# A decoder layer on one core: a third pair in seven products in three more units, with part of the low halves made by DMA

## The chip, the cores and the metric

One core of a Trainium2 chip runs one launch of the whole layer. The metric is the device time of that launch in microseconds (us).

## What is computed

```python
# x: 1 x 256 x 2048, fp32; D_MODEL 2048, SEQ 256, D_FF 5632
xn = rms(x)
p  = xn @ w_in                                   # all columns of both mixers, gates included
h  = x + (sigmoid(gA) * (fox(p) @ w_up_fox) + sigmoid(gB) * (nsa(p) @ w_up_nsa)) @ w_out
y  = h + (silu(rms(h) @ w_ffn_gate) * (rms(h) @ w_ffn_up)) @ w_ffn_down
```

FoX is attention with a forget gate (8 heads); NSA is attention with compressed, selected and windowed keys. The change touches the start of the program, the product with `w_out`, and the first of the three groups of `w_ffn_down`.

## The kernel before

**Products in two halves.** All is fp32 to the last digits: each operand is split into a high part `hi` (rounded by ACT) and a low part `lo` (the rest, by DVE), and one product of 128x128 by 128x512 is three matmuls: high by high (L1167), high by low (L1168), low by high (L1169). The attention part has the same in L199 to L201.

**Pairs.** From the merge gates on, the work is a list of items, each a `Pair`: 256 rows of a weight by 1024 columns (two tiles of 128 rows, two halves of 512 columns). SP loads it raw (`load`, L1116), `split` (L1119 to L1145) makes its high and low parts, and PE multiplies it with the transposed activations. A plain pair takes 8 products, which is 24 matmuls (`mm_plain`). A pair whose number is in `sevens` takes 7 products, 21 matmuls, by Strassen's scheme in Winograd's form (`mm_seven`, banks m1 to m7). For these DVE makes sums of the weight's quarters (L1126, L1128, L1129) and two low parts (L1145), and ACT two high parts (L1143, L1136). A pair in `thin` has the low part of its second half made without DVE: ACT writes minus the high part into `lo` (L1138), and a DMA that POOL issues adds the weight onto it from memory (L1139); DVE makes the other half, 128x1024.

**Units.** `unit` (L1174) takes an order of eight pairs (six in the first group of `w_ffn_down`) that add up in the same banks of the PSUM. There are four "acc" banks, handed out in turn, for m1, m5, m6, m7 and for transposes, and four "m" banks for the rest. After the last pair in seven products `combine` (L1204) takes the acc banks to SBUF, with ACT and DVE (L1209 to L1213); after the last item `last` adds the m banks (L1223) and `done` takes the result on. `hooks` names work that goes in front of an item, (j, 0), or into the middle of a plain one, (j, 1).

**Transposes.** Activations are transposed on PE (L1084, four of 128x128 a pair) into an acc bank. `put_plain` takes the bank out for a plain pair: ACT writes the high part (L1044), DVE the low (L1045). `put_seven` does so for a pair in seven products, with sums: three passes of ACT (L1060, L1066, L1073) and five of DVE (L1067, L1069, L1070, L1071, L1076). `put_m` transposes for `w_out`, `hid_pair` for `w_ffn_down`.

**Order.** Each engine does its instructions in the order of the program. `run_ffn` keeps three raw pairs and four split parts ahead, and places loads and splits at an item's start and half way through an item in seven products. Nothing sets the order but this code and the tables that the change edits: `ORDER` and `THIN` (L1406 to L1408), `SD` (L1347), the call of `unit` for `w_out` (L1337 to L1341) and its hooks. `swiglu` sets its product (`mult`, L1363) two items later, `down` the store of a second unit three items later, as DMAs that add into `hacc` in memory (L1378).

**Start.** `awake(n)` (L249) multiplies the identity with itself n times, for PE to be at work before its operands are there; then come the first transposes (`transpose_gain`, L279) of x and the first products of the attention part (L199 to L201).

Of the kernel before, what the change touches and what calls it, by code (L numbers as in the profile page):

```python
# [9 lines left out]
F32R = mybir.dt.float32r  # L10
# [4 lines left out]
P = 128  # L15
# [39 lines left out]
def hybrid_block(ctx: ExitStack, tc: tile.TileContext, x, norm_attn, w_in, fox_f_bias,  # L55
# [193 lines left out]
    def awake(n):  # L249

        tp = bank("tp")
        for _ in range(n):
            nc.tensor.matmul(tp[:, 0:P], ident, ident, start=True, stop=True)

    awake(5)
    tp = bank("tp")
    nc.tensor.transpose(tp[:, 0:16], vna, ident[:16, :16])
    nc.vector.tensor_copy(vecT[:, 0:16], tp[:, 0:16])
# [666 lines left out]
    mT = [None] * 8  # L925
    msrc = {}
    here = [0]
# [84 lines left out]
    def home(key, kp, sevens):  # L1012

        four = len(sevens) == 4
        if four and key == 1:
            if kp in sevens:
                halves[key, kp] = u8(ypool, [P, 2, 8, P], F32R)
                return halves[key, kp][:, :, 0:7]  # L1020
            if kp == 7:
                return tuple(halves[key, o][:, :, 7] for o in sevens)
        if kp in sevens:
            return u8(ypool, [P, 2, 8, P], F32R)
        if four:
            return p3([P, 2, 2, T], "hp", 4, F32R) if kp == 7 else p3([P, 2, 2, T], "x4", 3, F32R)
        if kp == 4:
            return u8(ypool, [P, 2, 2, T], F32R)
        if kp in (1, 3):
            if (key, 1) not in halves:  # L1030
                halves[key, 1] = u8(ypool, [P, 2, 2, 2, T], F32R)
            return halves[key, 1][:, kp // 2]
        return p3([P, 2, 2, T], "x4", 3, F32R)
# [209 lines left out]
    def two(w, r0, c0):  # L1243
        return lambda kp: [w[r0 + kp * 2 * P:r0 + (kp + 1) * 2 * P, c:c + 512] for c in (c0, c0 + 512)]
# [45 lines left out]
    def put_m(kp, where):  # L1290
# [3 lines left out]
                                    kp % 2 * 256, kp, SW, where=where)  # L1294
        return put

    SX = (0, 1, 2, 3)
    unit((4, 5, 0, 6, 1, 2, 3, 7), (0, 1, 3), two(w_in, 0, OFF_GA + 1024), x_pair((0, 1, 3)), ga_evac(1),
         thin=(6, 7))
# [20 lines left out]
    def put_hs(kp, j):  # L1320

        return {(j + o // 2, o % 2): lambda o=o: put_h(kp + o) for o in range(4)}

    def h_evac(i):
        def done(c):
            hs[i] = dict(c)
            for t, h in ((0, 0), (1, 0), (0, 1), (1, 1)):
                row_ssq(hss[:, t, 2 * i + h:2 * i + h + 1], c[t, h])
                nc.gpsimd.dma_start(hacc[t * P:(t + 1) * P, (2 * i + h) * 512:(2 * i + h + 1) * 512], c[t, h])
        return done  # L1330
# [4 lines left out]
        rstd_from(rh, s2[:, :NT], D)  # L1335

    for i in range(2):  # L1337
        unit(range(8) if i else (1, 3, 0, 2, 5, 6, 4, 7), SW if i else SW[:2], two(w_out, 0, i * 1024),
             lambda kp: mT[kp], h_evac(i),
             put_hs(0, 5) if i else {(1, 0): put_m(5, "acc"), (1, 1): put_m(6, "acc"), (4, 1): put_m(4, "acc"),  # L1340
                                     (5, 1): put_m(7, "acc")}, add_rows(x, i * 1024))  # L1341


    hid = {}
    hsrc = {}
    GROUPS = ((0, 3), (3, 7), (7, 11))
    SD = ((0, 2), (0, 2, 4, 6), (0, 2, 4, 6))  # L1347

    def hid_pair(f, a, g):
        f0, f1 = GROUPS[g]  # L1350
# [18 lines left out]
    def down(g, i):  # L1369
        final = g == len(GROUPS) - 1  # L1370

        def store(c):
            for t, h in ((0, 0), (1, 0), (0, 1), (1, 1)):
                rows, cols = slice(t * P, (t + 1) * P), slice((2 * i + h) * 512, (2 * i + h + 1) * 512)
                if final:
                    nc.sync.dma_start(out[rows, cols], c[t, h])
                else:
                    nc.gpsimd.dma_start(hacc[rows, cols], c[t, h], accum_op=ALU.add)  # L1378

        def done(c):  # L1380
            if final or not i:
                store(c)
            else:
                after.append((here[0] + 3, lambda c=dict(c): store(c)))
        return done, add_rows(hacc, i * 1024) if final else None

    def transposes(f, j):

        return {j if isinstance(j, tuple) else (j, 1): lambda: [hid_pair(f, o, g_of[f]) for o in range(2)]}
# [7 lines left out]
    def down_unit(g, i, order, hooks, thin=()):  # L1397
# [5 lines left out]
             lambda kp: hid[f0 + kp // 2, kp % 2], done, hooks, add, thin, True)  # L1403

    g_of = {f: g for g, (f0, f1) in enumerate(GROUPS) for f in range(f0, f1)}
    ORDER = ((range(6), range(6)), ((0, 7, 2, 1, 4, 3, 6, 5), (0, 7, 2, 1, 4, 6, 3, 5)),  # L1406
             ((0, 1, 2, 4, 3, 5, 6, 7), (0, 1, 2, 4, 3, 6, 5, 7)))
    THIN = (((), ()), ((3, 5), (3, 5)), ((1,), ()))  # L1408
    for g, (f0, f1) in enumerate(GROUPS):
        more = g + 1 < len(GROUPS)  # L1410

        for f in range(f0 + (1 if g else 0), f1 + (1 if more else 0)):
            gate_up(f, transposes(f - 1, (7, 0)) if f > f0 + (1 if g else 0) else
                    {} if f else {(2, 0): h_rms, **put_hs(4, 3)})
        hooks = ({}, transposes(f1, 6 if g else 4)) if more else (transposes(f1 - 1, 4), {})
        for o in range(2):
            down_unit(g, o, ORDER[g][o], hooks[o], THIN[g][o])

# [10 lines left out]
    def split_next():  # L1429
        nonlocal nsplit  # L1430
        split(stream[nsplit])
        nsplit += 1
        if nsplit == 1:
            transpose_gain(xT[0], xin, 0, VA, (0, 1))

    def run_att(i, ch):
        nonlocal nload
# [121 lines left out]
```

## Time and profile before

| | |
|---|---|
| runs (us) | 1415.89, 1417.41, 1419.33; median 1417.41 |
| the profiled execution | 1419.76 us, its span 1418.0 us |
| PE busy | 1409.3 us, 99% of the span |
| DVE, ACT busy | 1206.9 us (85%), 854.0 us (60%) |
| POOL busy | 121.5 us (9%) |
| weights and activations by SP's queue | 273.77 MB, 59.0% of the 16 DMA engines' time |
| by POOL's queue | 35.47 MB, 14.5% |

Busy shares are means over the program. PE works nearly without a pause, so the time is the sum of what PE is given plus its short waits; the other engines count only where PE waits for them. In the timelines a matmul of 128x512 shows some 0.39 us from issue to its end, but the next starts 0.227 us after it: what it costs is the distance of two starts.

### The profile page before, as it was taken

To read this page: it belongs to the slowest core of one execution; us is meant where nothing else is said; L and a number is where in the kernel's file an instruction comes from. 1 tells how busy PE (TensorE), PEld (TensorE's weight loads), DVE (VectorE), ACT (ScalarE), POOL (GpSimd) and SP (SyncE) were. 2 spreads that over 40 slices of the span, in tenths; PEclk is the share of its full clock that TensorE was granted. 3 is DMA by queue.
4 is the path that set the end of the run, shared out by engine and by line. 5 is a ranking of instruction groups with operands and counts; after the bars stand their busy time and mean duration, and the time that the engine had idled before them with its cause. 6 is when DMAs were issued, how large, how long until landed. Compare 5 with 4: busy or idle time off the path is not lost.

```text
span 1418.0 us, 18071 instructions
## 1 busy us (share of the span) xinstructions
PE 1409.3 (99%) x6507; PEld 1165.4 (82%) x6507; DVE 1206.9 (85%) x1566; ACT 854.0 (60%) x1080; POOL 121.5 (9%) x126
## 2 busy tenths in 40 slices
PE   9999999999999999999999999999999999999998
PEld 7888878888888888888888888888888888788887
DVE  5687877777767897879898999898999998899996
ACT  5556554556666665655665666556666666666643
POOL 0111000000000000100110000002010011110000
PEclk9999999999999999999999999999999999999999
DMA  7677877454434798777777778689878698978785
GB/s 261 202 222 204 262 244 211 137 165 136 147 119 149 248 256 253 202 229 233 226 226 233 212 237 264 203 223 284 226 238 252 200 242 256 264 230 248 222 243 158
DMA packets 177142, 310.67 MB, mean 219 GB/s; under 512 B 12910, under 2 KB 42188, under 8 KB 176924
## 3 DMA queue, kind: packets, MB, share of 16 engines
q1 hardware_dynamic: 159100, 273.77, 59.0%
q0 software_dynamic: 17776, 35.47, 14.5%
q8 instruction: 51, 0.84, 0.2%
q10 hardware_dynamic: 176, 0.27, 0.1%
q14 instruction: 39, 0.32, 0.1%
HBM read 301.07 MB, written 8.40 MB: 218 GB/s over the span
## 4 chain that ended last, share of the span: by engine, by line
PE 81%; DVE 7%; issue 6%; DMA 4%; ACT 1%; POOL 0%; SPq 0%; DVEq 0%; POOLq 0%; ACTq 0%
PE m L1168 11%; PE m L1167 11%; PE m L1169 11%; PE acc L199 9%; PE acc L201 9%; PE acc L200 9%; PE acc L1167 4%; PE acc L1168 4%; PE acc L1169 4%; DVE lo L1145 3%; DMA raw<-in_w_ffn_down_dram 2%; PE m L558 1%; DVE sums L1126 1%; DMA raw<-in_w_ffn_up_dram 1%; PE acc L1084 1%
## 5 line engine op out<-in xcount | busy, mean ns | idle before, releaser
L1145 DVE TENSOR_TENSOR lo<-raw,hi 128x1536 fp32r<-128x1536 f32 (+2 forms) x168 | 299.9, 1787 | 26.8 <-ACT hi L1141 14.3
L1143 ACT ACTIVATE hi<-raw 128x1536 fp32r<-128x1536 f32 (+1 forms) x125 | 208.1, 1668 | 87.4 <-PE m L1169 40.3
L175 DVE TENSOR_TENSOR hl<-raw,hl 128x1024 fp32r<-128x1024 f32 (+2 forms) x157 | 187.5, 1202 | 74.4 <-ACT hl L174 72.6
L1136 ACT ACTIVATE hi<-sums 128x1024 fp32r<-128x1024 f32 x154 | 161.3, 1060 | 147.5 <-PE m L1169 59.5
L199 PE MATMUL acc<-hl,u 128*128 128x512 f32 (+1 forms) x544 | 217.2, 399 | 0.2
L201 PE MATMUL acc<-hl,u 128*128 128x512 f32 (+1 forms) x544 | 212.2, 390 | 0.0
L200 PE MATMUL acc<-hl,u 128*128 128x512 f32 (+1 forms) x544 | 211.6, 389 | 0.0
L174 ACT ACTIVATE hl<-raw 128x1024 fp32r<-128x1024 f32 (+2 forms) x157 | 160.5, 1042 | 62.7 <-PE acc L201 48.3
L1145 DVE TENSOR_TENSOR lo<-sums,hi 128x2048 fp32r<-128x2048 f32 x77 | 175.9, 2284 | 5.9 <-ACT hi L1136 5.7
L1168 PE MATMUL m<-lo,hp 128*128 128x512 f32 x368 | 143.8, 391 | 2.3 <-DMA lo<-in_w_ffn_up_dram 2.0
L1167 PE MATMUL m<-hi,hp 128*128 128x512 f32 x368 | 144.1, 392 | 0.0
L1169 PE MATMUL m<-hi,hp 128*128 128x512 f32 x368 | 143.3, 389 | 0.0
L1167 PE MATMUL m<-hi,u 128*128 128x512 f32 x321 | 125.2, 390 | 0.0
L1169 PE MATMUL m<-hi,u 128*128 128x512 f32 x321 | 124.9, 389 | 0.0
L1168 PE MATMUL m<-lo,u 128*128 128x512 f32 x321 | 124.9, 389 | 0.0
L199 PEld LDWEIGHTS acc<-hl,u 128*128 128x128 f32 x544 | 102.7, 189 | 21.9 <-ACT u L281 0.5
L201 PEld LDWEIGHTS acc<-hl,u 128*128 128x128 f32 x544 | 102.5, 188 | 21.6 <-DVE u L282 0.4
L200 PEld LDWEIGHTS acc<-hl,u 128*128 128x128 f32 x544 | 102.7, 189 | 19.3
L1126 DVE TENSOR_TENSOR sums<-raw 128x1024 f32<-128x1024 f32 x71 | 86.5, 1219 | 2.5 <-DMA raw<-in_w_ffn_down_dram 2.1
L1168 PEld LDWEIGHTS m<-lo,hp 128*128 128x128 f32 x368 | 69.1, 188 | 18.3 <-DMA lo<-in_w_ffn_up_dram 3.8
L1141 ACT ACTIVATE hi<-raw 128x2048 fp32r<-128x2048 f32 x43 | 81.8, 1902 | 0.0
L1169 PEld LDWEIGHTS m<-hi,hp 128*128 128x128 f32 x368 | 69.1, 188 | 14.2
(336 smaller groups left out, 2641.4 us busy)
## 6 DMA issues: line engine op xcount, KB each, us to landing
raw<-in_w_in_dram SPq DMA_DIRECT2D x111, 512.0 KB
raw<-in_w_ffn_gate_dram SPq DMA_DIRECT2D x88, 512.0 KB
raw<-in_w_ffn_up_dram SPq DMA_DIRECT2D x88, 512.0 KB
raw<-in_w_ffn_down_dram SPq DMA_DIRECT2D x88, 512.0 KB
lo<-in_w_ffn_up_dram POOLq DMA_DIRECT2D x30, 512.0 KB, 7.2
raw<-in_w_out_dram SPq DMA_DIRECT2D x28, 512.0 KB
raw<-in_w_in_dram SPq DMA_DIRECT2D x32, 384.0 KB
raw<-in_w_up_fox_dram SPq DMA_DIRECT2D x16, 512.0 KB
```

The costliest lines, as they stand in the source:

```text
L174: nc.scalar.activation(hi[:, :m], ch.raw[:, :m], AF.Copy)
L175: nc.vector.tensor_tensor(lo[:, :m], ch.raw[:, :m], hi[:, :m].bitcast(F32), op=ALU.subtract)
L199: nc.tensor.matmul(o, h, ch.hi[:, j], start=first and j == 0, stop=False)
L200: nc.tensor.matmul(o, h, ch.lo[:, j], start=False, stop=False)
L201: nc.tensor.matmul(o, l, ch.hi[:, j], start=False, stop=last and j == w - 1)
L1126: nc.vector.tensor_tensor(s[:, 0:2], w[:, 0].unsqueeze(1).to_broadcast([P, 2, 512]), w[:, 1:4:2], op=ALU.add)
L1136: nc.scalar.activation(hi[:, o:o + 2], src[:, o:o + 2], AF.Copy)
L1143: nc.scalar.activation(h, src, AF.Copy)
L1145: return lambda: nc.vector.tensor_tensor(l, src, h.bitcast(F32), op=ALU.subtract)
L1167: nc.tensor.matmul(o, h, hi, start=n == 0, stop=False)
L1168: nc.tensor.matmul(o, h, lo, start=False, stop=False)
L1169: nc.tensor.matmul(o, l, hi, start=False, stop=n + 1 == total[key])
```

## The change

It makes a third pair of `w_out`'s first unit a pair in seven products (kp 4), and a third pair (kp 4) in both units of the first group of `w_ffn_down`. The orders of these units change with it, and three pairs of each become thin: kp 5, 6, 7 and kp 1, 3, 5. The transposes for `w_out` are done in two pairs of pairs, 5 and 4 ahead of the second item, 6 and 7 in its middle, where 4 and 7 were done at the fifth and sixth item. kp 4's transposed copy gets a buffer of another pool ("h8"). At the start one multiplication by `awake` is added to the first five, and one after the first two transposes. The store of a second down unit is set five items later, where it was three, and the transposes of the first group's next pair one item later.

```diff
-    awake(5)
+    awake(6)
...
+        if key == "m" and kp == 4:
+            return p3([P, 2, 8, P], "h8", 2, F32R)
         if kp in sevens:
             return u8(ypool, [P, 2, 8, P], F32R)
...
+    def put_ms(*kps):
+        return lambda: [put_m(kp, "acc")() for kp in kps]
...
-        unit(range(8) if i else (1, 3, 0, 2, 5, 6, 4, 7), SW if i else SW[:2], two(w_out, 0, i * 1024),
-             lambda kp: mT[kp], h_evac(i),
-             put_hs(0, 5) if i else {(1, 0): put_m(5, "acc"), (1, 1): put_m(6, "acc"), (4, 1): put_m(4, "acc"),
-                                     (5, 1): put_m(7, "acc")}, add_rows(x, i * 1024))
+        unit(range(8) if i else (1, 3, 0, 5, 2, 4, 6, 7), SW, two(w_out, 0, i * 1024), lambda kp: mT[kp], h_evac(i),
+             put_hs(0, 5) if i else {(1, 0): put_ms(5, 4), (1, 1): put_ms(6, 7)}, add_rows(x, i * 1024),
+             () if i else (5, 6, 7), True)
...
-    SD = ((0, 2), (0, 2, 4, 6), (0, 2, 4, 6))
+    SD = ((0, 2, 4), (0, 2, 4, 6), (0, 2, 4, 6))
...
-                after.append((here[0] + 3, lambda c=dict(c): store(c)))
+                after.append((here[0] + 5, lambda c=dict(c): store(c)))
...
-    ORDER = ((range(6), range(6)), ((0, 7, 2, 1, 4, 3, 6, 5), (0, 7, 2, 1, 4, 6, 3, 5)),
+    ORDER = (((0, 1, 2, 4, 3, 5),) * 2, ((0, 7, 2, 1, 4, 3, 6, 5), (0, 7, 2, 1, 4, 6, 3, 5)),
-    THIN = (((), ()), ((3, 5), (3, 5)), ((1,), ()))
+    THIN = (((1, 3, 5),) * 2, ((3, 5), (3, 5)), ((1,), ()))
...
-        hooks = ({}, transposes(f1, 6 if g else 4)) if more else (transposes(f1 - 1, 4), {})
+        hooks = ({}, transposes(f1, 6 if g else 5)) if more else (transposes(f1 - 1, 4), {})
...
         if nsplit == 1:
             transpose_gain(xT[0], xin, 0, VA, (0, 1))
+            awake(1)
```

In the rows that follow, the numbers behind a name are buffers; lines of the changed kernel are two higher than before from L1024 to L1290, and four to five higher later. PE's queue at the start, before and with the change (`ident` is the identity, `u` a tile of x, `acc` the first products' banks):

```order
L253 MATMUL m_106<-ident 128x128 x5
L257 MATMUL m_112<-ident,vna 128x16
L253 MATMUL m_115<-ident 128x128 x3
L279 MATMUL m_158<-ident,u_1_83 128x128
L279 MATMUL m_158<-ident,u_2_84 128x128
L279 MATMUL m_163<-ident,u_1_83 128x128
L279 MATMUL m_163<-ident,u_2_84 128x128
L199 MATMUL acc_182<-hl_155,u_6_119 128x512
```
```order
L253 MATMUL m_106<-ident 128x128 x6
L257 MATMUL m_113<-ident,vna 128x16
L253 MATMUL m_116<-ident 128x128 x3
L279 MATMUL m_159<-ident,u_1_83 128x128
L279 MATMUL m_159<-ident,u_2_84 128x128
L279 MATMUL m_164<-ident,u_1_83 128x128
L279 MATMUL m_164<-ident,u_2_84 128x128
L253 MATMUL m_169<-ident 128x128
L199 MATMUL acc_185<-hl_156,u_6_120 128x512
```

One identity product more stands ahead of everything, and one between the first transposes and the first product.

DVE's queue in the first unit of `w_out`, about its second and third item, before and with the change (`x_1013` and then `x_1014` are kp 5's transposed copy, `x_1019` and then `x_1023` kp 6's, `x_1025` kp 7's, `h_1016` kp 4's; `lo` are low parts of weights, `sums` the sums for seven products):

```order
L1045 TENSOR_TENSOR x_1013_5806<-acc_5801,x_1013_5806 128x512
L1126 TENSOR_TENSOR sums_5811<-u_989_5623 128x1024
L1128 TENSOR_TENSOR sums_5811<-sums_5811,u_989_5623 128x512
L1129 TENSOR_TENSOR sums_5811<-sums_5811,u_989_5623 128x512
L1145 TENSOR_TENSOR lo_1015_5810<-u_989_5623,hi_1014_5809 128x1536
L1045 TENSOR_TENSOR x_1019_5837<-acc_5832,x_1019_5837 128x512
```
```order
L1047 TENSOR_TENSOR x_1014_5809<-acc_5804,x_1014_5809 128x512
L1069 TENSOR_TENSOR F_5819<-F_5818 128x256
L1071 SCALAR_TENSOR_TENSOR F_5819<-F_5819,F_5818 128x128
L1072 TENSOR_TENSOR h_1016_5817<-F_5818,h_1016_5817 128x512
L1073 TENSOR_TENSOR F_5819<-F_5818,F_5819 128x128
L1078 TENSOR_TENSOR h_1016_5817<-F_5819,h_1016_5817 128x512
L1147 TENSOR_TENSOR lo_1020_5829<-u_990_5626,hi_1019_5828 128x1024
L1047 TENSOR_TENSOR x_1023_5854<-acc_5849,x_1023_5854 128x512
L1047 TENSOR_TENSOR x_1025_5862<-acc_5857,x_1025_5862 128x512
```

Where a weight's sums and low part stood between kp 5's copy and kp 6's, kp 4's `put_seven` and kp 5's halved low part stand now, and kp 7's copy comes right behind.

DVE's queue where the first unit of `w_ffn_down` begins, before and with the change (`u_1331` before and `u_1335` now are kp 4's transposed copy, the `L1223` and `L1225` rows the unit before it being added up):

```order
L1045 TENSOR_TENSOR u_1331_7726<-acc_7721,u_1331_7726 128x512
L1045 TENSOR_TENSOR x_1333_7734<-acc_7729,x_1333_7734 128x512
L1223 TENSOR_TENSOR qs_7683<-m_7484,qs_7683 128x512
L1223 TENSOR_TENSOR qs_7684<-m_7488,qs_7684 128x512
L1223 TENSOR_TENSOR q_1326_7685<-m_7492,q_1326_7685 128x512
L1223 TENSOR_TENSOR q_1327_7686<-m_7530,q_1327_7686 128x512
L1145 TENSOR_TENSOR lo_1335_7738<-raw_1316_7627,hi_1334_7737 128x2048
L1126 TENSOR_TENSOR sums_7776<-raw_1319_7648 128x1024
```
```order
L1069 TENSOR_TENSOR F_7743<-F_7742 128x256
L1071 SCALAR_TENSOR_TENSOR F_7743<-F_7743,F_7742 128x128
L1072 TENSOR_TENSOR u_1335_7741<-F_7742,u_1335_7741 128x512
L1073 TENSOR_TENSOR F_7743<-F_7742,F_7743 128x128
L1078 TENSOR_TENSOR u_1335_7741<-F_7743,u_1335_7741 128x512
L1047 TENSOR_TENSOR x_1339_7757<-acc_7752,x_1339_7757 128x512
L1225 TENSOR_TENSOR qs_7698<-m_7499,qs_7698 128x512
L1225 TENSOR_TENSOR qs_7699<-m_7503,qs_7699 128x512
L1225 TENSOR_TENSOR q_1330_7700<-m_7507,q_1330_7700 128x512
L1225 TENSOR_TENSOR q_1331_7701<-m_7545,q_1331_7701 128x512
L1147 TENSOR_TENSOR lo_1341_7761<-raw_1320_7642,hi_1340_7760 128x1024
L1128 TENSOR_TENSOR sums_7801<-raw_1323_7663 128x1024
```

kp 4's copy takes five passes instead of one, and kp 1's low part is half as wide.

## Rows read from the trace of the kernel before

**Rows 1.** The page: span; busy time, share and instructions of each engine.
```profile
span 1418.0 us, 18071 instructions
...
PE 1409.3 (99%) x6507; PEld 1165.4 (82%) x6507; DVE 1206.9 (85%) x1566; ACT 854.0 (60%) x1080; POOL 121.5 (9%) x126
```

**Rows 2.** Timeline of PE, last unit: start, busy, operation, out<-in [idle before <-releaser].
```profile
1397.62 0.39 PE L1167 MATMUL acc<-hi,u 128*128 128x512 f32 x1
...
1402.38 0.39 PE L1167 MATMUL m<-hi,x 128*128 128x512 f32 x1
...
1407.82 0.39 PE L1167 MATMUL m<-hi,hp 128*128 128x512 f32 x1
```

**Rows 3.** Timeline of PE and its weight loads (PEld), start of the program.
```profile
1.43 2.50 PE L253 MATMUL m<-ident 128*128 128x128 f32 x10 [1.43 <-POOL ident masks.py:199]
...
6.72 0.29 PEld L199 LDWEIGHTS acc<-hl,u 128*128 128x128 f32 x1 [0.54 <-ACT u L281]
...
6.72 0.80 PE L199 MATMUL acc<-hl,u 128*128 128x512 f32 x1
...
10.66 0.40 PE L199 MATMUL acc<-hl,u 128*128 128x512 f32 x1
```

**Rows 4.** Timeline of PE, first unit of `w_out`, about its third item.
```profile
637.41 0.60 PE L1084 MATMUL acc<-ident,qs 128*128 128x128 f32 x4
637.76 0.48 PE L1167 MATMUL m<-hi,u 128*128 128x512 f32 x1
...
646.54 0.39 PE L1167 MATMUL acc<-hi,u 128*128 128x512 f32 x1
...
647.36 0.50 PE L1167 MATMUL acc<-hi,u 128*128 128x512 f32 x1
```

**Rows 5.** Timeline of DVE: kp 5's copy, then a `put_seven` later in the unit.
```profile
641.77 0.68 DVE L1045 TENSOR_TENSOR x<-acc,x 128x512 fp32r<-128x512 f32 x1
...
661.71 0.42 DVE L1067 TENSOR_TENSOR F<-F 128x256 f32<-128x256 f32 x1
...
664.57 1.22 DVE L1126 TENSOR_TENSOR sums<-raw 128x1024 f32<-128x1024 f32 x1
```

**Rows 6.** Timeline of ACT: its last pass of that `put_seven`; a thin pair's passes.
```profile
663.29 0.63 ACT L1073 ACTIVATE u<-F 128x512 fp32r<-128x512 f32 x1 [2.68 <-DVE F L1071]
...
949.02 1.05 ACT L1138 ACTIVATE lo<-raw 128x1024 fp32r<-128x1024 f32 x1
949.97 1.90 ACT L1141 ACTIVATE hi<-raw 128x2048 fp32r<-128x2048 f32 x1
```

**Rows 7.** Timeline of DVE, first unit of `w_ffn_down`.
```profile
886.81 1.28 DVE L1223 TENSOR_TENSOR qs<-m,qs 128x512 f32<-128x512 f32 x2
...
892.03 1.22 DVE L1126 TENSOR_TENSOR sums<-raw 128x1024 f32<-128x1024 f32 x1
...
898.50 2.28 DVE L1145 TENSOR_TENSOR lo<-raw,hi 128x2048 fp32r<-128x2048 f32 x1
900.70 1.41 DVE L1363 SCALAR_TENSOR_TENSOR q<-q,rh,qs 128x512 f32<-128x512 f32 x2
```

**Rows 8.** Timeline of PE: first low part of that unit.
```profile
889.25 0.39 PE L1168 MATMUL acc<-lo,u 128*128 128x512 f32 x1
```

**Rows 9.** Timeline of POOL and PE: a thin pair's DMA after two seven items; its use.
```profile
596.80 1.19 POOL L1139 DMA_DIRECT2D lo<-in_w_in_dram  x1 [16.64 <-ACT lo L1138]
...
605.76 0.39 PE L1168 MATMUL m<-lo,u 128*128 128x512 f32 x1
```

**Rows 10.** Landing times of the thin pairs' DMAs, issue to landing.
```profile
DMA to landing us min/median/max: 5.6/7.7/10.2
```

**Rows 11.** Waits of PE for thin pairs' DMAs, whole program: us, times, longest.
```profile
PE m L1168 <- DMA lo<-in_w_ffn_up_dram: 2.0, 2, 1.6
```

**Rows 12.** Windows, first down group: us, PE, PEld, DVE, ACT, POOL, PEclk, DMA share, GB/s.
```profile
886.00:946.00 60.00, 60.00 (x271) 49.78 (x270) 55.24 (x48) 31.33 (x26) 3.45 (x4) 1.00 0.76 222
```

**Rows 13.** The page: POOL's DMA queue: packets, MB, share of 16 engines.
```profile
q0 software_dynamic: 17776, 35.47, 14.5%
```

## The prediction

> **What bounds the kernel now.** I read the page first. PE is busy for 1409.3 of 1418.0 us [rows 1], so the time is the number of matmuls times their distance, plus the few places where PE stands still. The distance is read from the starts of three items in a row at the program's end [rows 2]: an item in seven products takes 1402.38 − 1397.62 = 4.76 us for 21 matmuls, a plain one 1407.82 − 1402.38 = 5.44 us for 24; both give 0.227 us a matmul. The other engines matter only where PE waits for them, and there is little of that: PE's longest wait for a thin pair's DMA is 1.6 us and all such waits make 2.0 us in two places, though 45 thin pairs are made before the change [rows 11]. So two things count: the matmuls that go, and every new wait that the edits open. Which these are the order of the instructions shows; how long each takes, the timelines.
>
> 0.2% of this time is 2.8 us, about what a measurement of this kernel can tell from no change.
>
> **Products.** Three pairs go from eight products to seven: 3 × (5.44 − 4.76) = **−2.04** [rows 2]. PE gets nothing else for it, since a pair's transposes are four of 128x128 either way. All of it lies on the path, as PE is the path.
>
> **First unit of `w_out`.** Before, PE stood still once at its third item: m6's first matmul should have followed m7's after 3 × 0.227, at 647.22, and began at 647.36 [rows 4], behind kp 6's copy on DVE. That wait of **−0.14** goes with the place. The new order opens a larger one. The eight transposes of kp 4 and kp 7 now stand in front of the third item, 0.35 for four [rows 4], so m7 starts at 646.54 + 0.70 = 647.24. (They go from a later place, so their own cost is nil.) m7's acc bank is the one that kp 6's transposes used, and DVE's copy of kp 6 stands behind kp 4's `put_seven` and the thin kp 5. Now the chain. DVE is through with kp 5's copy at about 641.77 + 0.60 = 642.37 [rows 5]. A `put_seven` takes DVE 664.57 − 661.71 = 2.86 [rows 5]; ACT's last pass of it ends 663.29 + 0.63 − 661.71 = 2.21 after its start [rows 5, 6], here at 644.58. Then ACT makes the thin pair's two passes, 949.97 − 949.02 = 0.95 and up to 1.90 [rows 6], to about 647.35. Only then can DVE make kp 5's low half, half of the 2.28 of a full one [rows 7], so to 648.5, and only then kp 6's copy, 0.68 [rows 5], to 649.2. PE waits from 647.24 to 649.2: **+1.95**. The bounds: nothing, if ACT's passes slip in front, which its order does not allow; or 0.6 more, if kp 7's copy, next on DVE, holds the next bank too. I take the chain as it stands, since every link has a row. Queued behind the waiting matmul is all of PE; the loads behind on SP run ahead of it and lose nothing.
>
> The rest of that unit has slack. DVE's added sums and second low part are paid for by the halves that DVE no longer makes. The accumulators are taken out two items before the unit's end where it was four, about 10 us, and the next unit asks for its first m bank a few products later; I cost this at nothing, with PE's waits at other unit ends as cover.
>
> **First group of `w_ffn_down`.** In its first unit DVE gets kp 4's `put_seven` in place of one copy, 2.86 against 0.60, so the unit before is added up from 886.81 + 2.26 = 889.07 on, four additions of 0.60 to 891.47 [rows 5, 7]. kp 1's low half takes 1.13, to 892.60; kp 2's sums and both its low parts 898.50 − 892.03 = 6.47 [rows 7], to 899.07; kp 4's sums and first low part the same without the last 2.20 (the distance of 898.50 and 900.70), to 903.34; `mult`'s two, 1.41 less a tail of 0.08, to 904.67; kp 4's second low part 2.28, to 906.95 [rows 7]. PE's first low part of the unit was used at 889.25 [rows 8]; kp 4's fourth product, the first to use that second part, comes one seven, one plain and one seven item and three products later: 889.25 + 4.76 + 5.44 + 4.76 + 3 × 0.68 = 906.25 [rows 2, 8]. Late by **+0.7**. The bounds are 0, if the additions overlap by their tails, and 1.4, if the second unit repeats it; there no unit's tail and no `mult` stands in the chain, so I take 0.7 once.
>
> **Thin pairs.** Nine more DMAs of POOL, which adds 9 × 1.2 us of issuing [rows 9] to an engine that is 9% busy [rows 1]. Each lands in 5.6 to 10.2 us, 7.7 in the middle [rows 10]. One that is issued with two seven items ahead of its use had 605.76 − 596.80 = 8.96 of lead [rows 9], others a plain item more or some 2 more. I cost them at nothing; if the cover goes, rival three has the price. In POOL's queue a store of `hacc` may stand behind them; its reader is the last unit, hundreds of us later.
>
> **Store and transposes later.** The store is told to go two items later, but each engine's rows come in the same order whether three or five stands there: it is put off to a point that the next unit's end settles anyway. Cost nil; this part doesn't do what it says. The later transposes are the same eight, with the acc banks freed before them.
>
> **Start.** From the first product to where distances become 0.227, nine matmuls take 10.66 − 6.72 = 3.94 us, 0.44 each [rows 3], the lower of the two clock levels (1.2 GHz), where the upper would take 2.04: a loss of 1.90. PE had been at work from 1.43, with a pause of 0.54 just ahead of the first product [rows 3]. The change puts a product of the identity into that pause; ten entries of it took 2.50 us and made five products [rows 3], so one is 0.5. Another 0.5 goes in front, of which a part lies in a pause behind it; the first product is later by 0 to 0.5, say 0.25. If without the pause the upper level is there at the first product, 1.90 − 0.25 = 1.65 is gained; with one product still slow, **−1.4**. The bounds are −1.9 and +0.25.
>
> The Trainium skill ("TensorE: Matmul & The Clock Gate", Part 1) says that the count of slow matmuls at a kernel's start differs from run to run of the same kernel. By it the filled pause would buy nothing that can be counted on, and the sum would be rival one's; the one profile here cannot show it, since it holds one start.
>
> **Sum.** −2.04 − 0.14 + 1.95 + 0.7 = +0.47 without the start, −0.93 with it. The profiled execution's 1419.76 would become 1418.8; it lies 2.35 above the median of the runs, and against the median of 1417.41 the forecast is **1416.5 us**: what the products save, the new waits take back.
>
> **Rivals.**
> *One: the level rises when it did.* The first products are then 0.25 late at half speed, +0.13: +0.6 in all, **1418.0**. For it: 5 us of work on PE before the first product had not raised the level [rows 3]. Against it: the pause is the only one left there.
> *Two: the waits are smaller and the start is worth all.* Half the bank wait (0.97), none in `w_ffn_down`, −1.9 at the start: −2.04 − 0.14 + 0.97 − 1.9 = −3.1, **1414.3**. For it: PE's row of waits has nothing as long as my 1.95 that isn't a DMA's [rows 11], and I added busy times that overlap by their tails. Against it: ACT's two passes for the thin pair lie bare in the chain.
> *Three, slower: the low halves land late.* In the first down group the 16 DMA engines are busy for 0.76 of 60 us, 45.6 us [rows 12]. POOL's queue spends 14.5% of 1418.0 us on 35.47 MB [rows 13], so 0.524 MB cost about 3.0 us of all 16, and six more make 63.8 us, over 60. Then landings pass the lead of 8.96 [rows 9], as the longest, 10.2, already does [rows 10]. Three of the nine (kp 6 of `w_out`, both kp 3) have this short lead; late by the longest wait seen, 1.6 each [rows 11], that is +4.8 on the forecast: **1421.3**. It decides once landings pass 9 us. Against it: 45 such DMAs cost 2.0 us so far, and the raw loads run ahead.
> The Trainium skill ("DMA: Bandwidth & Descriptors", Issuing engines are not separate DMA queues) says that transfers started by different engines share the same 16 DMA engines and interleave. By that rule POOL's transfers get no way of their own, and the case is rival three's; no row here shows nine more of them.
>
> **How the numbers follow.** The forecast has 0.40, rival one 0.23, two 0.25, three 0.12. Forecast and rival one lie within 0.2%: 0.63. Faster 0.25 and slower 0.12 are the other two. The range, 1413.3 to 1420.6, takes in forecast and rival one with the bounds of their waits, most of rival two (down to a unit below its value, where the start gives all and the bank wait goes too) and leaves out most of rival three.
>
> **What would show it.** In the profile after: 1360 matmuls in each of L1167 to L1169 where there were 1363; a start of m7 in `w_out`'s first unit about 2 us late, with DVE's L1047 as releaser; a wait of under 1 us for L1147 in the first down unit; at the start, products 0.227 apart from the first or second on. Waits for DMA `lo` from `w_out` or `w_ffn_down` would show rival three; slow products as before, rival one; no wait at m7, rival two. I am wrong in kind if PE waits anywhere else for more than 1 us.

## The result and the profile after

The changed kernel takes 1431.63 us (median of 6), the kernel before, on the same chip, 1418.34: a ratio of 1.0098 with a 95% interval of 1.0084 to 1.0112, so **13.9 us slower** (1.0098 times 1418.34; the two medians themselves differ by 13.3). The prediction was 1416.5, no measurable change, with a range up to 1420.6: wrong.

The two profiled executions differ by less, 1430.07 against 1419.76, because the one of before was an unusually long execution of its kernel and the one after the shortest of its six. The page after, against [rows 1, 13]:

```profile
span 1428.4 us, 18119 instructions
...
PE 1408.8 (99%) x6502; PEld 1162.8 (81%) x6502; DVE 1211.2 (85%) x1582; ACT 868.9 (61%) x1097; POOL 132.2 (9%) x135
...
q0 software_dynamic: 20224, 40.19, 16.4%
```

PE is as busy as before and the span is 10.4 us longer: the time went into waits. PE's waits in the whole program, after (before: 2.0 us for thin pairs' DMAs [rows 11], 0.3 for DVE's low parts, and the first 1.4 for the identity):

```profile
PE m L1170 <- DVE lo L1147: 3.2, 4, 2.0
PE acc L1169 <- DVE x L1047: 3.0, 2, 1.7
PE m L1170 <- DMA lo<-in_w_ffn_down_dram: 2.8, 2, 2.0
PE m L253 <- POOL ident masks.py:199: 1.4, 1, 1.4
PE m L1170 <- DMA lo<-in_w_ffn_up_dram: 1.4, 3, 0.6
PE acc L1170 <- DVE lo L1147: 1.2, 2, 1.0
PE m L1170 <- DMA lo<-in_w_out_dram: 1.0, 1, 1.0
PE m L1169 <- ACT hi L1143: 0.9, 1, 0.9
```

Without the identity's these make 13.5 us in 15 waits where there were 2.3 in 4. A wait costs some 0.27 more than its row says: m7 below stands for 1.72 but begins 1.88 late, and the next matmul follows it after 0.34, not 0.227. So the balance of the two profiles nearly closes: 11.2 more of waits and 11 × 0.27, less 2.04 for the products and 1.14 at the start, is an estimate of 11.0 for the 10.4 measured. The timeline of PE after, those of its matmuls that waited longest, from `w_out`'s first unit to the unit behind the first group of `w_ffn_down`:

```profile
648.16 0.50 PE L1169 MATMUL acc<-hi,u 128*128 128x512 f32 x1 [1.72 <-DVE x L1047]
...
669.36 0.50 PE L1170 MATMUL m<-lo,x 128*128 128x512 f32 x1 [0.96 <-DMA lo<-in_w_out_dram]
...
684.60 0.50 PE L1170 MATMUL m<-lo,u 128*128 128x512 f32 x1 [1.98 <-DVE lo L1147]
...
910.83 0.50 PE L1170 MATMUL acc<-lo,u 128*128 128x512 f32 x1 [1.04 <-DVE lo L1147]
...
945.11 0.49 PE L1169 MATMUL m<-hi,u 128*128 128x512 f32 x1 [0.89 <-ACT hi L1143]
946.37 0.50 PE L1170 MATMUL m<-lo,u 128*128 128x512 f32 x1 [0.76 <-DVE lo L1147]
951.40 0.50 PE L1170 MATMUL m<-lo,u 128*128 128x512 f32 x1 [2.02 <-DMA lo<-in_w_ffn_down_dram]
...
963.86 0.50 PE L1169 MATMUL acc<-hi,h 128*128 128x512 f32 x1 [1.28 <-DVE x L1047]
```

The first and the fourth are the two waits that the prediction costed (1.95 and 0.7). The other six are not in its sum: two in `w_out`, three in the second unit of `w_ffn_down`, one at the start of the unit behind it. Two of them, 1.98 and 1.28, are longer than 1 us at places that the prediction does not name, which by its own sign is wrong in kind. Two stretches of the other engines show where they come from. First POOL and DVE after, at the end of `w_out`'s first unit:

```profile
666.64 0.89 POOL L1252 DMA_DIRECT2D qs<-in_x_dram  x1 [2.48 <-DVE q L1212]
...
675.50 0.69 DVE L1225 TENSOR_TENSOR qs<-m,qs 128x512 f32<-128x512 f32 x1 [0.67 <-DMA qs<-in_x_dram]
677.54 0.69 DVE L1225 TENSOR_TENSOR qs<-m,qs 128x512 f32<-128x512 f32 x1 [1.34 <-DMA qs<-in_x_dram]
679.61 0.69 DVE L1225 TENSOR_TENSOR q<-m,q 128x512 f32<-128x512 f32 x1 [1.38 <-DMA q<-in_x_dram]
681.65 0.69 DVE L1225 TENSOR_TENSOR q<-m,q 128x512 f32<-128x512 f32 x1 [1.35 <-DMA q<-in_x_dram]
682.26 2.28 DVE L1147 TENSOR_TENSOR lo<-raw,hi 128x2048 fp32r<-128x2048 f32 x1
```

The DMAs that add x are issued once the accumulators are out, from 666.64 on (before from 654.80 on, and there no addition waited for them). The four additions stand still for them, and the next unit's low part, for which PE waits until 684.60, is queued behind them on DVE. Second, pieces of the chain of waits after, in the second unit of `w_ffn_down` (start, us, what):

```profile
927.76 14.05 DMA raw<-in_w_ffn_down_dram
...
942.20 0.06 ACT lo L1140
...
943.16 1.91 ACT hi L1143
945.09 1.24 DVE lo L1147
```

A raw load takes 14 us; ACT, which sat idle for it, starts kp 3's passes only at 942.20, so the high part, the low part and kp 3's own DMA are late one after the other: the waits at 945, 946 and 951.

### The profile page after: what moved, and what is told of

The parts are those of the page before. It is cut to its first block, busy times and chain, and to the rows that moved or that the text cites. A ratio compares the mean times of both kernels' runs of the same rounds, so it can differ in the third digit from the quotient of the medians.

```text
span 1428.4 us, 18119 instructions
## 1 busy us (share of the span) xinstructions
PE 1408.8 (99%) x6502; PEld 1162.8 (81%) x6502; DVE 1211.2 (85%) x1582; ACT 868.9 (61%) x1097; POOL 132.2 (9%) x135
## 3 DMA queue, kind: packets, MB, share of 16 engines
q1 hardware_dynamic: 159100, 273.77, 58.3%
## 4 chain that ended last, share of the span: by engine, by line
PE 79%; DVE 10%; DMA 7%; issue 3%; ACT 2%; SPq 0%; POOL 0%; DVEq 0%; ACTq 0%; POOLq 0%
PE m L1170 11%; PE m L1171 11%; PE m L1169 11%; PE acc L199 9%; PE acc L201 9%; PE acc L200 9%; DVE lo L1147 5%; PE acc L1169 4%; PE acc L1171 4%; PE acc L1170 4%; DMA raw<-in_w_ffn_down_dram 2%; DMA raw<-in_w_ffn_up_dram 2%; PE m L558 1%; DMA lo<-in_w_ffn_up_dram 1%; DVE sums L1128 1%
## 5 line engine op out<-in xcount | busy, mean ns | idle before, releaser
L1147 DVE TENSOR_TENSOR lo<-raw,hi 128x1024 fp32r<-128x1024 f32 (+2 forms) x168 | 289.5, 1725 | 34.2 <-ACT hi L1143 20.9
L1138 ACT ACTIVATE hi<-sums 128x1024 fp32r<-128x1024 f32 x160 | 168.4, 1062 | 150.7 <-DVE sums L1128 77.0
L1145 ACT ACTIVATE hi<-raw 128x1536 fp32r<-128x1536 f32 (+1 forms) x117 | 191.2, 1638 | 73.1 <-PE m L1171 27.7
L1147 DVE TENSOR_TENSOR lo<-sums,hi 128x2048 fp32r<-128x2048 f32 x80 | 182.8, 2285 | 3.1 <-ACT hi L1138 3.1
L1170 PE MATMUL m<-lo,u 128*128 128x512 f32 x300 | 117.1, 390 | 4.8 <-DVE lo L1147 2.7
L1169 PE MATMUL m<-hi,u 128*128 128x512 f32 x300 | 117.1, 390 | 0.9 <-ACT hi L1143 0.9
L1171 PE MATMUL m<-hi,u 128*128 128x512 f32 x300 | 116.8, 389 | 0.0
L1143 ACT ACTIVATE hi<-raw 128x2048 fp32r<-128x2048 f32 x51 | 97.1, 1903 | 0.0
L1128 DVE TENSOR_TENSOR sums<-raw 128x1024 f32<-128x1024 f32 x75 | 91.6, 1221 | 2.7 <-DMA raw<-in_w_ffn_down_dram 2.1
L1169 PE MATMUL acc<-hi,u 128*128 128x512 f32 x208 | 81.4, 391 | 1.7 <-DVE x L1047 1.7
```

The costliest lines, as they stand in the source:

```text
L1128: nc.vector.tensor_tensor(s[:, 0:2], w[:, 0].unsqueeze(1).to_broadcast([P, 2, 512]), w[:, 1:4:2], op=ALU.add)
L1138: nc.scalar.activation(hi[:, o:o + 2], src[:, o:o + 2], AF.Copy)
L1145: nc.scalar.activation(h, src, AF.Copy)
L1147: return lambda: nc.vector.tensor_tensor(l, src, h.bitcast(F32), op=ALU.subtract)
L1169: nc.tensor.matmul(o, h, hi, start=n == 0, stop=False)
L1170: nc.tensor.matmul(o, h, lo, start=False, stop=False)
```

## Experiments

Each ratio is to the kernel before on the same chip. In kernels made from the one before, the line numbers behind the edit are those of that kernel or two higher.

**The parts alone.** *The start:*

```diff
-    awake(5)
+    awake(6)
...
             transpose_gain(xT[0], xin, 0, VA, (0, 1))
+            awake(1)
```

> The kernel before with the two additions to awake and nothing else. In the trace after, a matmul late in the attention part starts 1.14 us earlier than before (16.92 for 18.06), although the first product starts 0.42 later. If the start's gain carries to the end and is the same in every execution: 1.1 us faster, about 1417.2 against 1418.3. If the level of the clock at the start differs from execution to execution and this was one lucky one: no difference on average, and a wider spread of the runs.

Measured 1416.41, ratio 0.9992 (0.9983 to 1.0000): the expected 1.1 us, at the edge of what can be told. But the profiles of the eleven kernels of this study without this edit (before, and ten below) show that the nine slow products of before [rows 3] are no fixed cost: one more, e13, has them, two have three slower ones, and seven have the first products 0.23 to 0.34 us apart. e13, and one of the seven, e11:

```profile
6.71 0.80 PE L199 MATMUL acc<-hl,u 128*128 128x512 f32 x1
...
10.67 0.40 PE L199 MATMUL acc<-hl,u 128*128 128x512 f32 x1
```

```profile
6.59 0.50 PE L199 MATMUL acc<-hl,u 128*128 128x512 f32 x1 [0.35 <-ACT u L281]
6.93 0.40 PE L200 MATMUL acc<-hl,u 128*128 128x512 f32 x1
7.16 0.45 PE L201 MATMUL acc<-hl,u 128*128 128x512 f32 x1
```

and the changed kernel:

```profile
7.14 0.70 PE L199 MATMUL acc<-hl,u 128*128 128x512 f32 x1
7.68 0.39 PE L200 MATMUL acc<-hl,u 128*128 128x512 f32 x1
```

The tenth product begins at 10.66 and 10.67 where nine are slow, at 8.67 to 8.96 in the seven, and at 8.55 to 9.52 in the five profiles with the edit. So the edit saves 1.1 us or more against a slow start, and in four of its five profiles loses 0.3 to 0.9 against another. None of the five has a run of nine slow products, but none against two of eleven doesn't show that the edit prevents them. The second comparison, e12 against e11, gives 0.6 us by the ratios, inside the intervals. That the edit gains is not shown.

*The first unit of `w_out`:*

```diff
+        if key == "m" and kp == 4:
+            return p3([P, 2, 8, P], "h8", 2, F32R)
...
-        unit(range(8) if i else (1, 3, 0, 2, 5, 6, 4, 7), SW if i else SW[:2], ...
+        unit(range(8) if i else (1, 3, 0, 5, 2, 4, 6, 7), SW, ...
+             put_hs(0, 5) if i else {(1, 0): put_ms(5, 4), (1, 1): put_ms(6, 7)}, add_rows(x, i * 1024),
+             () if i else (5, 6, 7), True)
```

> The kernel before with the new first unit of w_out alone (order, third seven, hooks, thin pairs, kp 4's buffer). The stage shift between the traces there is +4.5 us: three new waits of PE (1.9 for kp 6's copy, 1.2 for the thin pair's DMA, 2.2 for the next unit's low part behind the additions of x) less three matmuls' 0.68 and what is drawn ahead. Theory that the stages add up: 1422.8. Theory that a late stage is caught up later (the traces show both kernels' distance constant behind it): nearer 1418.3.

Measured 1424.59, ratio 1.0046 (1.0035 to 1.0057), +6.5: more than the stage's shift, and nothing is caught up.

*The first group of `w_ffn_down`:*

```diff
-    SD = ((0, 2), (0, 2, 4, 6), (0, 2, 4, 6))
+    SD = ((0, 2, 4), (0, 2, 4, 6), (0, 2, 4, 6))
...
-    ORDER = ((range(6), range(6)), ...
+    ORDER = (((0, 1, 2, 4, 3, 5),) * 2, ...
-    THIN = (((), ()), ((3, 5), (3, 5)), ((1,), ()))
+    THIN = (((1, 3, 5),) * 2, ((3, 5), (3, 5)), ((1,), ()))
...
-        hooks = ({}, transposes(f1, 6 if g else 4)) if more else (transposes(f1 - 1, 4), {})
+        hooks = ({}, transposes(f1, 6 if g else 5)) if more else (transposes(f1 - 1, 4), {})
```

> The kernel before with the new first group of w_ffn_down alone (third seven, order, thin pairs, transposes). Stage shift between the traces: +8.1 us by the next group's start, and about -1.0 later, where old waits shrink. If the stages add up: 1418.3 + 7.1 = 1425.4. If part of this shift came from w_out's late start of the pipeline: clearly less.

Measured 1424.33, ratio 1.0040 (1.0028 to 1.0052), +5.7. The three parts sum to −1.1 + 6.5 + 5.7 = 11.1; with intervals of more than a microsecond each that agrees roughly with the 13.9 of the whole (11.9 to 15.9). The later store is in none of the three.

**`w_ffn_down`: DMA engines or DVE.** In the whole changed kernel:

```diff
-    THIN = (((1, 3, 5),) * 2, ((3, 5), (3, 5)), ((1,), ()))
+    THIN = (((), ()), ((3, 5), (3, 5)), ((1,), ()))
```

> The changed kernel with no thin pair in the first group of w_ffn_down; its third pair in seven products and its order stay. Theory DMA: the six added DMAs fill the 16 DMA engines between 905 and 955, so a raw load takes 14 us, and ACT (idle 4.6 us for it), POOL and PE follow; without them the waits for DMA lo of w_ffn_down and ACT's 4.6 us go, and at least 5 of the 8 us come back: 1426.5 or less. Theory DVE: the third seven's sums and low parts fill DVE, loads are only late because it frees buffers late; then six full low parts more, 6 x 1.1 us on DVE, make it slower: 1434 or more.

Measured 1428.90, ratio 1.0073 (1.0061 to 1.0085): 3.5 under the change by the ratios, between the theories. The group's waits for low DMAs are gone and ACT's for a raw load is 1.0. Waits for DVE stay or have grown; PE's longest in the whole program:

```profile
PE acc L1169 <- DVE x L1047: 3.5, 2, 1.8
PE acc L1170 <- DVE lo L1147: 2.6, 3, 1.2
PE m L1170 <- DVE lo L1147: 2.6, 4, 1.9
```

Two of these, 1.70 and 1.94, are `w_out`'s, as in the changed kernel, and 1.11 stands behind the group; the group's own and the one at the next unit's start make 3.5 where the change has 6.0. The longest are 1.18 for a low part (1.04 in the change) and 1.77 at the next unit's start (1.28). Windows of both, first the change, then e4 (us, PE, PEld, DVE, ACT, POOL, PEclk, DMA share, GB/s):

```profile
905.00:955.00 50.00, 45.28 (x197) 36.27 (x196) 41.93 (x41) 30.05 (x26) 9.58 (x9) 1.00 0.95 247
```
```profile
905.00:955.00 50.00, 48.43 (x215) 38.95 (x214) 48.69 (x43) 27.18 (x22) 3.56 (x4) 1.00 0.76 219
```

Each theory has a part: with six more DMAs the 16 engines are full (0.95), without them DVE is (48.7 of 50 us). Neither way gave room for a third seven. Next, on e3, only one of the six removed:

```diff
-    THIN = (((1, 3, 5),) * 2, ((3, 5), (3, 5)), ((1,), ()))
+    THIN = (((1, 3, 5), (3, 5)), ((3, 5), (3, 5)), ((1,), ()))
```

> e3_down with kp 1 of the second w_ffn_down unit no longer thin (one of the six added DMAs gone; DVE makes 1.1 us more). In the trace after, that DMA is issued at 924.6, four stores that add into hacc at 925 to 929, and the raw loads of 927.8 land only at 941.8. Theory DMA: a thin pair's DMA costs all 16 engines some 3 us, the raw loads land 2 to 3 us earlier, and the chain behind them (ACT idle, high part, low DMA: waits of 1.0, 1.0, 2.2) shrinks by 2 to 4 us: 1421 to 1422. Theory DVE: 1425 or more.

Measured 1422.01, ratio 1.0035 (1.0021 to 1.0049). The time alone doesn't separate it from e3, but the traces do. In e3 SP asks for kp 3's raw tile at 921.5 and ACT gets it at 936:

```profile
921.53 0.96 SPq L1116 DMA_DIRECT2D raw<-in_w_ffn_down_dram  x2
```
```profile
936.05 1.06 ACT L1138 ACTIVATE lo<-raw 128x1024 fp32r<-128x1024 f32 x1 [4.00 <-DMA raw<-in_w_ffn_down_dram]
```

In e7 (chain of waits, then ACT's timeline):

```profile
922.30 10.40 DMA raw<-in_w_ffn_down_dram
```
```profile
932.81 1.06 ACT L1138 ACTIVATE lo<-raw 128x1024 fp32r<-128x1024 f32 x1 [0.68 <-DMA raw<-in_w_ffn_down_dram]
```

One DMA of 0.5 MB less, and a raw load that took some 14 us takes 10.4: close to the 3.0 us that the prediction estimated a thin pair to cost all 16 engines. Theory DMA holds for the raw loads, by one profile each. With kp 3 of the second unit taken out too:

```diff
-    THIN = (((1, 3, 5), (3, 5)), ((3, 5), (3, 5)), ((1,), ()))
+    THIN = (((1, 3, 5), (5,)), ((3, 5), (3, 5)), ((1,), ()))
```

> e7_down_35 with kp 3 of the second w_ffn_down unit no longer thin either (kp 5 alone stays). Theory DMA: kp 3's own low DMA (wait 1.2, it has the short lead behind two seven items) and the load on the engines go; 1 to 2 us faster, about 1420.5. Theory DVE: DVE has 1.1 us more in a stretch where it was busy 9.8 of 10 us, kp 3's low part is late by as much, no gain: 1422 or more.

Measured 1421.05, ratio 1.0022 (1.0013 to 1.0031), 1.8 under e7 by the ratios, as theory DMA has it, though the intervals overlap; the wait for kp 3's low DMA (1.08 in e7) is gone. Of what is left, +3.1, the group's rows show only waits for DVE, 0.68, 0.34 and 0.24. They make 1.3, about what the two pairs save, so the rest stays open.

The transposes put back to the fifth item, on e3:

```diff
-        hooks = ({}, transposes(f1, 6 if g else 5)) if more else (transposes(f1 - 1, 4), {})
+        hooks = ({}, transposes(f1, 6 if g else 4)) if more else (transposes(f1 - 1, 4), {})
```

> e3_down with the transposes of the next group's first pair back at the fifth item (they are at the sixth in the change), ahead of ACT's passes for the next unit's thin pair. Theory that these transposes hold the acc banks when the next unit begins (wait of 1.3 at 956): that wait goes, and the time falls to 1423. Rival, that the accumulators are not out yet at the fifth item: PE waits at the transposes instead, 2 us or more, and the time stays or rises.

Measured 1424.45, ratio 1.0046 (1.0034 to 1.0058): the time stays, as the rival has it, but without its wait of 2 us. The wait at the next unit's start nearly goes (1.15 in e3, 0.2 here); PE waits at the transposes for DVE's L1210 instead (0.36) and for a low DMA behind them (0.44). Where these transposes stand makes no difference that the runs can tell.

**`w_out`: the bank, the thin pairs, x.** The transposes in another order, on e2:

```diff
-             put_hs(0, 5) if i else {(1, 0): put_ms(5, 4), (1, 1): put_ms(6, 7)}, add_rows(x, i * 1024),
+             put_hs(0, 5) if i else {(1, 0): put_ms(5, 6), (1, 1): put_ms(4, 7)}, add_rows(x, i * 1024),
```

> e2_w_out with the transposes in the order 5, 6 and then 4, 7 (it was 5, 4 and 6, 7), so that kp 6's bank is copied ahead of kp 4's put_seven and of the thin kp 5. Theory of the sum on record (m7's bank is held by kp 6's copy on DVE, behind ACT's thin passes): m7's wait of 1.9 falls to at most 0.5 (m6 may wait for kp 7's copy), the time to about 1423. Rival, that ACT and DVE are just late altogether at this place: the wait moves to the next product and the time stays at 1424.6.

Measured 1420.83, ratio 1.0020 (1.0011 to 1.0029), 3.7 under e2 by the ratios. m7's wait is gone and none takes its place at the third item: that the bank is held by kp 6's copy, behind kp 4's `put_seven` and kp 5's low part on DVE, is shown. The waits at the unit's end are as in e2. For those, first no thin pair at all, on e2:

```diff
-             () if i else (5, 6, 7), True)
+             (), True)
```

> e2_w_out with no thin pair in w_out's first unit. Theory that the wait at the unit's end (2.2 us, DVE waiting for the DMAs that add x) comes from the accumulators being taken out only two items before the end: it stays near 2, and the time falls only by the 1.1 of the thin pair's DMA wait and what ACT no longer does ahead of kp 6's copy, to about 1423. Theory that thin pairs' DMAs, issued at 660 and 663 just ahead of those of x, hold these up: the wait at the end falls under 0.7, and the time to 1421 or less, as long as DVE keeps up with three full low parts (3 x 1.1 us more).

Measured 1424.04, ratio 1.0042 (1.0027 to 1.0056), no different from e2. The end's wait fell from 2.0 to 0.7, but the additions still stood for x. m7's wait stays, 1.82: ACT's extra pass for a thin pair, a link of the prediction's chain, is not needed for it, since a full low part on DVE takes as long. Then kp 5 alone thin, on e6:

```diff
-             () if i else (5, 6, 7), True)
+             () if i else (5,), True)
```

> e6_w_out_order with kp 5 alone thin in w_out's first unit (kp 6 and 7 get full low parts from DVE). Their two DMAs were issued just ahead of those that bring x at the unit's end. Theory that the end's wait of 2.2 is lateness of x's DMAs among other transfers: as between e2 and e5, x lands 1.5 to 2 us earlier, the wait falls to about 0.9, the low DMA's wait of 0.9 goes: 1418.5. Theory that it is the two items alone, whatever else the engines move: only the 0.9 goes, 1420 or more. If DVE's 2.2 us more make kp 6's and kp 7's parts late: 1421 or more.

Measured 1419.96, ratio 1.0017 (1.0009 to 1.0026): 0.4 under e6 by the ratios, too little to tell. The low DMA's wait is gone and the one at the end stays, 2.1: the second theory. e5's smaller wait is for more than half a matter of PE's later arrival (682.35, in e2 681.63; the waits end at 683.05 and 683.65). With the start's additions, the diff of e1:

> e11 with the start's two additions. If stages add up: 1.1 us under e11, about 1417.4, no faster than before by what a measurement can tell; below e1_start's 1416.4 only if the third seven's 0.7 is not eaten by waits.

Measured 1419.75, ratio 1.0013 (1.0003 to 1.0024): the start adds nothing here that can be told. On e6, accumulators out three items before the end, not two:

```diff
-        unit(range(8) if i else (1, 3, 0, 5, 2, 4, 6, 7), SW, two(w_out, 0, i * 1024), lambda kp: mT[kp], h_evac(i),
+        unit(range(8) if i else (1, 3, 0, 2, 4, 5, 6, 7), SW, two(w_out, 0, i * 1024), lambda kp: mT[kp], h_evac(i),
```

> e6_w_out_order with the three pairs in seven products of w_out's first unit in a row (order 1, 3, 0, 2, 4, 5, 6, 7), so that the accumulators go out three items before the unit's end, not two. Theory that the unit's end waits for the DMAs of x because they are issued only two items ahead of it: they come 5.4 us earlier, the wait of 2.2 goes, the time falls by about 2, to 1418.5. Rival, that three sevens in a row are more than DVE can feed (6.6 us of sums and low parts for 4.76 us of PE): a wait for a low part inside the unit takes its place, and the time stays at 1420.8 or rises.

Measured 1430.60, ratio 1.0086 (1.0073 to 1.0099): the rival, and worse. Waits of 2.5 for a transposed copy (L1047), 1.1 for a low part and 5.3 for two low DMAs: DVE frees raw buffers too late (SP stands for its low part up to 16.8 us, in e6 10.2), and then waits for the load itself:

```profile
673.22 1.22 DVE L1128 TENSOR_TENSOR sums<-raw 128x1024 f32<-128x1024 f32 x1 [6.47 <-DMA raw<-in_w_out_dram]
```

Last, the DMAs of x taken away from e11, which leaves x out of these columns:

```diff
-             put_hs(0, 5) if i else {(1, 0): put_ms(5, 6), (1, 1): put_ms(4, 7)}, add_rows(x, i * 1024),
+             put_hs(0, 5) if i else {(1, 0): put_ms(5, 6), (1, 1): put_ms(4, 7)}, add_rows(x, i * 1024) if i else None,
```

> e11_w_out_5 without the four DMAs that add x to the first unit's 1024 columns (the residual of these columns is left out of the output). Theory that the end of w_out's first unit waits because DVE stands behind the landing of these DMAs, with the next unit's low part queued behind it: the wait of 2.3 at 678 goes, 1417.5, and L1225 has no DMA as releaser. Rival, that DVE's own work (three pairs' sums, the accumulators, kp 6's and kp 7's parts) is late there by as much: a wait of over 1 stays, 1419 or more.

Measured 1418.55, ratio 1.0005 (0.9997 to 1.0014), 1.7 under e11 by the ratios. PE has no wait at the unit's end, and DVE's additions no releaser:

```profile
674.08 1.28 DVE L1225 TENSOR_TENSOR qs<-m,qs 128x512 f32<-128x512 f32 x2
675.28 1.28 DVE L1225 TENSOR_TENSOR q<-m,q 128x512 f32<-128x512 f32 x2
676.47 2.29 DVE L1147 TENSOR_TENSOR lo<-raw,hi 128x2048 fp32r<-128x2048 f32 x1
```

So the wait is x's. And without it a third seven in `w_out` is still no faster than two.

**Two mends together**, in the whole changed kernel: e6's order and e10's thin pairs, the same two lines:

```diff
-             put_hs(0, 5) if i else {(1, 0): put_ms(5, 4), (1, 1): put_ms(6, 7)}, add_rows(x, i * 1024),
+             put_hs(0, 5) if i else {(1, 0): put_ms(5, 6), (1, 1): put_ms(4, 7)}, add_rows(x, i * 1024),
...
-    THIN = (((1, 3, 5),) * 2, ((3, 5), (3, 5)), ((1,), ()))
+    THIN = (((1, 3, 5), (5,)), ((3, 5), (3, 5)), ((1,), ()))
```

> The whole changed kernel with two mends: transposes in the order 5, 6 and 4, 7 (as e6), and thin pairs 1, 3, 5 in the first and 5 alone in the second unit of w_ffn_down (as e10). If the parts are independent: 1431.6 less 3.6 less 3.2, 1424.8, still slower than before by 7. If the w_out stage's lateness was also what made the down group late: under 1423.

Measured 1426.64, ratio 1.0053 (1.0038 to 1.0069): it brings back 6.4 of the 13.9 by the ratios, nearer to independence (6.8) than to the other reading. In its profile the waits at `w_out`'s end (1.97), in the first down unit (1.12) and at the next unit's start (2.02) stay. No version here beats the kernel before clearly; the start alone is the only one below it.

## Why the prediction was wrong

- **Products, −2.04.** Right and small: the profile after has 1360 matmuls in each of the three lines where there were 1363, and kp 4's item in `w_out` takes 4.76 us (660.52 to 665.28). No time brings it to light, since each third seven opens waits of its own size or more.
- **The wait for kp 6's copy, +1.95.** Right: m7 began 1.88 late (648.16, after 646.05 and 0.227), behind kp 6's copy as named; e6 took it away. Only the part of ACT's thin pass in it is not shown (e5).
- **The first unit of `w_ffn_down`, +0.7.** Right in place and cause (DVE's low part at 910.83), 1.04 of wait for 0.7.
- **Start, −1.4.** The profile agreed (the 40th product at 17.71 for 18.85, 1.14 earlier), the medians hardly: a loss of 1.90 as in [rows 3] came in two of eleven profiles. The Trainium skill ("TensorE: Matmul & The Clock Gate", Part 1) had it right, that the count of slow matmuls at the start differs from run to run: it was nine, three, or one at most in the eleven profiles here. The pause alone does not decide it (its 0.54 is the weight loads' idle time, on PE's own row it is 0.14): e6 begins its first product at 6.72, behind the same rows as before, and has no run of slow ones. With 1.90 twice, 0.7 and 0.4, the mean loss is an estimate of 0.45 us, so this term was mis-sized: by these profiles about half a microsecond was there to be gained. That the slow products ran at the lower level is read from their distance, 0.43, which is that of e6 at a granted clock of 0.55 (below); the profile's own granted clock reads 1.00 there.
- **"I cost this at nothing, with PE's waits at other unit ends as cover"** is the first step that failed. It asked only who needs the banks next. The accumulators out two items before the end bring x's DMAs so late that DVE stood for them until 681.65, and DVE's queue holds the next unit's low part behind these additions: 1.98 in the profile after, gone in e13. The prediction's own rule, to name what is queued behind a waiting instruction, was not applied to DVE.
- **"Thin pairs. I cost them at nothing"** is the second, and by the waits the larger. Rival three had the price of such a DMA about right, 3 us of all engines, and its main victim wrong. The low DMAs' landings hardly moved (5.7, 7.4 and 10.5 against [rows 10]); the raw loads' did (ACT's longest wait for one in this group is 4.6, 2.4 before). What the window of 60 us hid is that the surplus collects in the second unit, where the four stores of the first unit into `hacc` run as well. Windows after, and the same ten microseconds before (us, PE, PEld, DVE, ACT, POOL, PEclk, DMA share, GB/s):

```profile
935.00:945.00 10.00, 9.22 (x41) 7.31 (x39) 5.30 (x5) 4.93 (x5) 1.20 (x1) 1.00 0.99 281
```
```profile
935.00:945.00 10.00, 10.00 (x49) 8.34 (x49) 9.86 (x11) 6.43 (x6) 0.00 (x0) 1.00 0.80 276
```

  Before, the DMA engines are full ahead of this window (0.94 from 925 to 935) and ease in it; after, they go on, 0.99 for 0.80. ACT and DVE go from 6.4 and 9.9 to 4.9 and 5.3: they wait. The Trainium skill ("DMA: Bandwidth & Descriptors", Issuing engines are not separate DMA queues) says that transfers of all engines share the 16 and interleave; 14 us for a raw load among the thin pairs' DMAs, 10.4 with one less, agree. Three waits, 3.67 together, follow.
- **Rival three**, +4.8, had 0.12; its direction was right, and two of its three places came: kp 6 of `w_out` waits 0.96 for its low DMA, kp 3 of the second unit 2.02, the latter because ACT's pass ahead of that DMA was late. Its sum was too low, since it counted late low halves alone.
- **Store and transposes later.** The transposes were not free where the change puts them: their copy stands behind ACT's passes for the next unit's thin pair (the 1.28 at 963.86). But e8 shows that the old place costs as much with the third seven. The later store does nothing, as predicted: e3 has the old one, and its four stores begin at 966.86, 9.13 after the matmul that waited at the next unit's start (957.73); after the change it is 972.99, also 9.13 after (963.86).

## What to carry to other kernels

Work moved from an engine to the DMA queues is costed by the loads that it delays, window by window of ten microseconds, not by its own landing; here a stretch with the 16 engines at 0.76 and DVE busy for 55.2 of 60 us [rows 12] took the third seven neither with six more DMAs nor with none. The share alone does not tell: from 905 to 955, e10, with four of the six, has 1.02 and waits of 1.0 us in the group and behind it, the whole change 0.95 and waits of 6.0. And where results are taken out closer to a unit's end, ask not only for the banks but for what the engine that waits there has queued behind: one late DMA held up a low part that had nothing to do with it.

## What the runs showed of the hardware

A wait of PE can cost more than its length. In e6, behind the wait of 2.0 us that ended at 681.73, the granted clock fell to the lower level (1.2 GHz) and came back at 685.9; windows of PE's row (columns as above):

```profile
679.00:682.00 3.00, 1.01 (x5) 0.55 (x4) 3.00 (x3) 1.45 (x3) 0.54 (x1) 1.00 1.04 371
682.00:684.00 2.00, 2.00 (x7) 1.51 (x7) 1.93 (x3) 1.81 (x2) 0.00 (x0) 0.59 1.05 411
684.00:686.00 2.00, 2.00 (x7) 1.56 (x6) 2.00 (x3) 1.37 (x2) 0.00 (x0) 0.55 1.04 349
686.00:688.00 2.00, 2.00 (x10) 1.65 (x9) 2.00 (x1) 1.62 (x1) 0.00 (x0) 1.00 0.85 280
```

Nine matmuls there take 3.65 us (682.31 to 685.96), up to 0.43 each, instead of 2.04: 1.6 us lost on top of the wait. The same stretch has it in e2, e11, e12 and e14, others in e4, e5, e8 and e14 (once each) and in e9 (twice), each in or behind a wait of 1.8 to 3.4 us. Others of that length had none: e3's of 2.1, e9's of 2.5, and the profile after, with three of 1.7 to 2.0.

The mean granted clock of the changed kernel's six executions is 1.0, 1.0, 0.999, 0.998, 0.998 and 0.997. Of such a mean some 2 us at the lower level lie behind the last matmul (e3 and e10 have 0.999 with no fall ahead of it). At 0.998 of 1431 us 5.7 us are at the lower level, so some 3.5 within the program, half of which is lost: an estimate of 1.8 us. So the executions at 0.998 and 0.997 probably had such a fall. But the six times don't go by it (1432.93 at 1.0, 1430.78 at 0.997), so it isn't shown to be why the medians lie further apart than the two profiled executions, nor why e2 lost more than its stage's shift.

A DMA that adds is dear for the 16 engines: 0.524 MB of POOL's queue cost them about 3.0 us [rows 13], and by the same division of the page of before a plain load of SP's queue of the same size costs 1.6 (59.0% of 1418.0 us for 273.77 MB). Both are estimates; POOL's queue holds the stores into `hacc` too.
